# A list scheduler written in the kernel books two more costs: a wait of VectorE for GpSimd, and the overhead of a float32r product

## The chip, the cores and the metric

One core of one Trainium2 chip runs the whole step. The metric is device time in microseconds (us), from launch to the last output; the median of three runs is compared.

## What is computed

One inference step of a one-layer trunk for two groups of tokens that share the weights: a prompt of 1024 tokens, and a sample of 64 tokens that continues from stored states. Cut to what matters here:

```python
cols = x @ w_in + b_in                        # 1088 x 1024 by 1024 x 9864, float32
a_cols, a_z, b_qk, b_v, b_i, b_f, b_o, b_z, c_q, c_k, c_v, c_z, gates = split(cols)
# A: RWKV-7, 8 heads of 64: one state per head, token after token
S = S * w_t + sa_t (kk_t * a_t)^T + v_t k_t^T ;  sa_t = -S kk_t ;  y_t = S r_t
# B: mLSTM, 4 heads of 128, in chunks with a running maximum
# C: stick-breaking attention, 8 heads of 64, with a product over the keys between
ys  = stack([ya * silu(a_z), yb * silu(b_z), yc * silu(c_z)])
mix = sum(sigmoid(gates) * (ys @ w_branch)) @ w_out
x   = layer_norm(alpha * x + mix)
x   = x + (p @ w_ple) * sigmoid(x @ w_ple_gate)
```

The outputs are the new x of both groups, and the states of A, B and C.

## The kernel before

**Main stream.** The large products run as sums of three float32r products (high part by high part, low by high, high by low), function `three`. The 1088 tokens are cut into three groups of 384, 384 and 320 columns. A block is 128 columns of `w_in`: 8 steps of the contraction by 3 products by 3 groups, 72 products. 78 such blocks (5,592 products, as one of them needs 48) are followed by the merge with `w_branch` and by the tail. The main stream writes the PSUM banks `bk0` to `bk2`, which the order of instructions shows as bk_65 to bk_67, and reads the tiles `xh`, `xl` and `whl`.

**Side tasks.** The three mixers are written as Python generators, called tasks, and yield one operation at a time. A comes first: `a_front` prepares a pair of heads (bonus sums over `bd`, squared norms, scores), `a_inverses` solves triangular systems on GpSimd, 60 tensor_tensor instructions in a row for each of eight inverses, and `a_chain` carries the state: 17 chunks of 64 tokens for each of four pairs of heads, 68 chunks in all. One chunk of the chain goes like this: two products give `ry` (the first reads `V2`); VectorE and ScalarE copy them into `R1`; a product `u` reads `R1`; VectorE negates `u` into `uv2`, and ScalarE into `U2`; a product `zz` reads `uv2`, and VectorE forms the next state from it; a last product of the chunk reads `U2`. B and C follow, and `m_prep` readies the merge.

**What sets the order.** Every engine runs its instructions in the order in which the program issues them. That order is made while the program is built, by class `Sched`, a list scheduler. It keeps a clock for each engine and books every operation with a cost: `mm`, `tr`, `act`, `tt`, `ts`, `stt` and `cp` hold these cost formulas. The main stream books its products one after the other. After each step of `three` (three products), `poll` lets every side task issue the operation that it holds, if `when` says that this operation could start by the clock of TensorE. A side product is thus put into TensorE's queue at the step of the main stream at which the planner believes its inputs to be ready. If they are late on the chip, TensorE stands still, with the main stream's products behind it. `SLACK` is 0 for TensorE, so no reserve is planned.

Of the kernel before, what the change touches and what calls it, by code (L numbers as in the profile page):

```python
# [28 lines left out]
class Buf:  # L29
    def __init__(self, heap, off, n):  # L30
        self.heap, self.ap, self.off, self.n = heap, heap.ap[:, off:off + n], off, n
# [84 lines left out]


class Op:
    __slots__ = ("eng", "cost", "reads", "writes", "fn", "q", "load")

    def __init__(self, eng, cost, reads, writes, fn, q, load):
        self.eng, self.cost, self.reads, self.writes, self.fn, self.q, self.load = eng, cost, reads, writes, fn, q, load


class Sched:
# [3 lines left out]
    def __init__(self):  # L129
        self.clk = {"pe": 0.0, "act": 0.0, "dve": 0.0, "pool": 0.0, "s": 0.0, "dma": 0.0}  # L130
        self.tasks = []
        self.cur = self.main = Task(None, "main", main=True)
        self.idle = 0.0
        self.mem = {}
        self.log = None
        self.cache = {}
        self.shade = 0.0

    def note(self, what):
        if self.log is not None:  # L140
            self.log.append((round(self.clk["pe"] / 1000), what))
# [45 lines left out]
    def execute(self, op, at=0.0):  # L187
        if op.q:
            st = max(self.clk[op.q], self.dep(op), at)
            self.clk[op.q] = st + QUEUE[op.q]  # L190
            end = self.clk["dma"] = max(st + 1100.0, self.clk["dma"]) + op.cost
            done = end + 900.0
        else:
            st = max(self.clk[op.eng], self.dep(op), at)
            if op.load:
                st = max(st, self.clk["pe"] + op.load[0] - self.shade)
                self.shade = op.load[1]
            end = done = st + op.cost
            if op.eng == "pe":
                self.idle += st - self.clk["pe"]  # L200
            self.clk[op.eng] = end
        e = ENG[op.eng]
        for m, p, f in op.reads:
            np.maximum(m[0][1, p, f], end, out=m[0][1, p, f])
        end = done
        for m, p, f in op.writes:
            m[0][0, p, f] = end
            m[1][p, f] = e
        return op.fn()

    def emit(self, eng, cost, reads, writes, fn, q=None, load=None):
        op = Op(eng, cost, [self.region(a) for a in reads], [self.region(a) for a in writes], fn, q, load)
        if self.cur.main:
            return self.execute(op, self.clk["pe"] if eng == "dma" else 0.0)
        return op
# [80 lines left out]
def psum(ap):  # L296
    return "PSUM" in str(ap.space).upper()


def fsize(ap):  # L300
    n = 1
    for s in ap.shape[1:]:
        n *= s
    return n


class K:
# [5 lines left out]
    def mm(self, out, lhsT, rhs, start, stop, more=False):  # L313
        n, w = fsize(out), 0.82 * fsize(lhsT)
        if lhsT.dtype == F32R:
            c = d = 1 + (213.0 if n < 256 else n / 2.4)
        else:
            d = 1 + 2 * n / 2.4
            c = d + max(d, w)
        return self.S.emit("pe", c, [lhsT, rhs], [out],  # L320
                           lambda: self.nc.tensor.matmul(out, lhsT, rhs, start=start, stop=stop, skip_group_check=more),  # L321
                           load=(w, d))
# [32 lines left out]
    def tt(self, out, a, b, op, e="v"):  # L355
        if e == "v":
            return self.S.emit("dve", fsize(out) * 1.04 + 68, [a, b], [out],
                               lambda: self.nc.vector.tensor_tensor(out=out, in0=a, in1=b, op=op))  # L358
        return self.S.emit("pool", fsize(out) * 2.1 + 150, [a, b], [out],
                           lambda: self.nc.gpsimd.tensor_tensor(out=out, in0=a, in1=b, op=op))  # L360

    def ts(self, out, a, s1, op0, s2=None, op1=None, e="v"):
        kw = {"op1": op1} if op1 is not None else {}
        rd = [a] + [x for x in (s1, s2) if x is not None and not isinstance(x, (int, float))]
        q = self.nc.vector if e == "v" else self.nc.gpsimd
        if e == "v":
            c = fsize(out) * (1.04 if psum(a) else 0.52) + 68 + 62 * (len(rd) - 1)
        else:
            c = fsize(out) * (1.05 if (op0, op1) == (OP.mult, OP.add) else 2.33 + len(rd)) + 180
        return self.S.emit("dve" if e == "v" else "pool", c, rd, [out],  # L370
                           lambda: q.tensor_scalar(out=out, in0=a, scalar1=s1, scalar2=s2, op0=op0, **kw))  # L371

    def stt(self, out, a, s, b, op0, op1):
        rd = [a, b] + ([] if isinstance(s, float) else [s])
        return self.S.emit("dve", fsize(out) * 1.04 + 68 + 62 * (len(rd) - 2), rd, [out],
                           lambda: self.nc.vector.scalar_tensor_tensor(out=out, in0=a, scalar=s, in1=b, op0=op0, op1=op1))  # L376

    def cp(self, out, in_, e="v"):
        if e == "v":
            return self.S.emit("dve", fsize(out) * (1.04 if psum(in_) else 0.52) + 68, [in_], [out],  # L380
                               lambda: self.nc.vector.tensor_copy(out, in_))  # L381
        return self.S.emit("pool", fsize(out) * 3.4 + 120, [in_], [out], lambda: self.nc.gpsimd.tensor_copy(out, in_))

    def tr32(self, out, in_):
# [1874 lines left out]
```

## Time and profile before

| | us |
|---|---|
| median of 3 runs | 1745.0 (1744.7 to 1746.75) |
| the profiled execution | 1746.5 |
| span of its instructions | 1744.8 |
| TensorE (PE) busy | 1698.2, 97% of the span |
| VectorE (DVE) busy | 1159.4, 66% |
| ScalarE (ACT) busy | 791.5, 45% |
| GpSimd (POOL) busy | 452.1, 26% |

The profile draws a float32r product longer than the distance to the next one, because products overlap in the array; a busy TensorE is therefore not one without any loss. The granted TensorE clock is at its upper level, 2.4 GHz, in nearly the whole span.

### The profile page before, as it was taken

Reading aid. Unit: us, or ns where it says so; the run is one execution under the profiler, and the core shown is the slowest. Engines: PE = TensorE matmul, PEld = TensorE weight load, DVE = VectorE, ACT = ScalarE, POOL = GpSimd, SP = SyncE. Lnnn points to the kernel's source line nnn. Section 1 sums busy time; section 2 is a strip of 40 time slices with the busy share of each in tenths; the row PEclk is TensorE's granted clock in tenths of the full one; section 3 lists DMA queues with packets and bytes.
Section 4 is the critical chain, followed back from the end, with each engine's and each line's share of the span. In section 5 each row is a group of like instructions: output and inputs, shape, how many; then the busy total and the mean of one; then the engine's idle time right before and its main releaser. Section 6 shows DMA issues by size and latency. Waiting matters only on the chain.

```text
span 1744.8 us, 29994 instructions
## 1 busy us (share of the span) xinstructions
PE 1698.2 (97%) x10849; PEld 1582.7 (91%) x10849; DVE 1159.4 (66%) x2682; ACT 791.5 (45%) x1823; POOL 452.1 (26%) x951
## 2 busy tenths in 40 slices
PE   6999998999999999999999999999999999999999
PEld 5999987888888999999999999999999999988787
DVE  8766577677777656866743476867685568787743
ACT  6444454545455445544443655555654312222421
POOL 6005547075547441321202111212220000000100
PEclk9999999999999999999999999999999999999999
DMA  5543432323332333545424433343324877631421
GB/s 160 194 130 98 108 100 67 100 72 102 100 92 81 91 88 117 162 122 161 136 86 123 141 108 110 97 114 103 88 80 127 255 225 248 208 131 51 149 82 54
DMA packets 224634, 212.09 MB, mean 122 GB/s; under 512 B 53540, under 2 KB 192598, under 8 KB 224486
## 3 DMA queue, kind: packets, MB, share of 16 engines
q1 hardware_dynamic: 197518, 169.50, 32.8%
q10 hardware_dynamic: 22552, 29.02, 4.7%
q0 software_dynamic: 4416, 11.66, 2.2%
q8 instruction: 85, 1.39, 0.3%
q14 instruction: 63, 0.52, 0.1%
HBM read 136.81 MB, written 73.36 MB: 120 GB/s over the span
## 4 chain that ended last, share of the span: by engine, by line
PE 85%; DVE 8%; ACT 4%; issue 1%; DMA 1%; ACTq 0%; SPq 0%; POOL 0%; DVEq 0%
PE bk L321 80%; PE bk L328 5%; ACT heap L353 3%; DVE heap L376 2%; DVE heap L358 2%; DVE heap L371 1%; DVE whl L358 1%; DMA heap<-in_x_prompt_dram 1%; ACT whl L353 1%; DMA out_c_p_dram<-heap 0%; DVE heap L412 0%; DVE xl L358 0%; ACTq L431 0%; DVE heap L381 0%; DVE heap L409 0%
## 5 line engine op out<-in xcount | busy, mean ns | idle before, releaser
L321 PE MATMUL bk<-xh,whl 128*128 128x384 f32 (+1 forms) x3768 | 1051.9, 339 | 0.3 <-DVE heap L376 0.3
L321 PEld LDWEIGHTS bk<-xh,whl 128*128 128x128 f32 x3768 | 679.6, 188 | 10.0 <-issue 3.8
L321 PE MATMUL bk<-xl,whl 128*128 128x384 f32 (+3 forms) x2184 | 669.1, 328 | 1.4 <-POOL xl L360 0.8
L321 PEld LDWEIGHTS bk<-xl,whl 128*128 128x128 f32 (+1 forms) x2184 | 405.3, 189 | 4.9 <-POOL xl L360 1.5
L353 ACT ACTIVATE heap<-bk 64x64 f32<-64x64 f32 (+9 forms) x679 | 217.4, 335 | 348.1 <-PE bk L321 131.3
L360 POOL TENSOR_TENSOR heap<-heap 32x30 f32<-32x30 f32 (+14 forms) x480 | 266.1, 554 | 36.5
L358 DVE TENSOR_TENSOR whl<-heap,whl 128x1024 fp32r<-128x1024 f32 (+1 forms) x114 | 122.2, 1075 | 114.3 <-ACT whl L353 113.8
L328 PE MATMUL bk<-ident,heap 128*128 128x128 f32 (+3 forms) x942 | 177.3, 277 | 14.5 <-ACT heap L353 12.6
L358 DVE TENSOR_TENSOR heap<-heap 128x256 f32<-128x256 f32 (+18 forms) x372 | 174.8, 475 | 15.4 <-DMA heap<-yz 6.9
L321 PE MATMUL bk<-heap 128*128 128x128 f32 (+6 forms) x954 | 166.6, 290 | 11.7 <-ACT heap L353 9.8
L321 PEld LDWEIGHTS bk<-heap 128*128 128x128 f32 (+3 forms) x954 | 125.9, 180 | 37.7 <-ACT heap L353 23.8
L353 ACT ACTIVATE heap<-bk,pc 128x384 f32<-128x384 f32 (+5 forms) x218 | 113.9, 548 | 94.1 <-PE bk L321 66.0
L328 PEld LDWEIGHTS bk<-ident,heap 128*128 128x128 f32 (+3 forms) x942 | 119.9, 142 | 30.2 <-issue 15.5
L353 ACT ACTIVATE heap<-heap 64x64 f32<-64x64 f32 (+9 forms) x330 | 113.1, 348 | 66.5 <-DVE heap L376 28.1
L353 ACT ACTIVATE whl<-heap 128x1024 fp32r<-128x1024 f32 (+1 forms) x116 | 105.4, 912 | 73.0 <-PE bk L321 37.8
L321 PE MATMUL bk<-heapr 128*128 128x256 f32 (+2 forms) x524 | 123.0, 335 | 0.0
L353 ACT ACTIVATE heap<-bk,hb 128x384 f32<-128x384 f32 (+1 forms) x120 | 67.5, 563 | 121.3 <-PE bk L321 96.6
L321 PE MATMUL bk<-heap,heap 32*32 32x32 f32 (+2 forms) x990 | 111.7, 243 | 8.8 <-ACT heap L353 7.0
L321 PEld LDWEIGHTS bk<-heap,heap 128*128 128x128 f32 (+1 forms) x990 | 90.1, 152 | 26.9 <-ACT heap L353 17.4
L321 PE MATMUL bk<-heapr,whl 128*128 128x384 f32 (+2 forms) x648 | 113.9, 335 | 0.6 <-DVE heap L376 0.6
L376 DVE SCALAR_TENSOR_TENSOR heap<-heap 128x4 f32<-128x4 f32 (+8 forms) x259 | 81.4, 316 | 47.8 <-ACT heap L353 42.1
L321 PEld LDWEIGHTS bk<-heapr,whl 128*128 128x128 f32 x648 | 108.3, 188 | 4.1 <-issue 0.8
(154 smaller groups left out, 1795.3 us busy)
## 6 DMA issues: line engine op xcount, KB each, us to landing
heap<-in_w_in_dram SPq DMA_DIRECT2D x77, 512.0 KB
heap<-gt SPq DMA_DIRECT2D x24, 544.0 KB
gt<-heap ACTq DMA_DIRECT2D x48, 192.0 KB
heap<-crd SPq DMA_DIRECT2D x12, 544.0 KB
heap<-yd SPq DMA_DIRECT2D x24, 272.0 KB
heap<-yz SPq DMA_DIRECT2D x24, 272.0 KB
heap<-in_w_branch_dram SPq DMA_DIRECT2D x24, 256.0 KB
xsd<-heap SPq DMA_DIRECT2D x24, 192.0 KB
```

Source lines behind the costliest of these rows:

```text
L321: lambda: self.nc.tensor.matmul(out, lhsT, rhs, start=start, stop=stop, skip_group_check=more),
L328: lambda: self.nc.tensor.transpose(out, in_, self.ident[:p, :p]), load=(0.82 * fsize(in_), d))
L353: return self.nc.scalar.activation(out, in_, func, **kw)
L358: lambda: self.nc.vector.tensor_tensor(out=out, in0=a, in1=b, op=op))
L360: lambda: self.nc.gpsimd.tensor_tensor(out=out, in0=a, in1=b, op=op))
L371: lambda: q.tensor_scalar(out=out, in0=a, scalar1=s1, scalar2=s2, op0=op0, **kw))
L376: lambda: self.nc.vector.scalar_tensor_tensor(out=out, in0=a, scalar=s, in1=b, op0=op0, op1=op1))
```

## The change

Two costs of the planner change, and nothing else. First, a float32r product (`mm`) is booked with 13 ns beside its columns, where it was 1 ns. Second, a VectorE operation of the kinds `tt`, `ts`, `stt` and `cp` that reads no PSUM operand carries a flag `port`. When such an operation would be booked to start while a GpSimd operation is booked as running, its start is moved to the end of that operation. `pool` keeps the last 64 booked intervals of GpSimd. The same instructions are issued, in another order.

```diff
+        self.pool = []
...
+            if op.port:
+
+                for a, b in reversed(self.pool):
+                    if a <= st < b:
+                        st = b
+                        break
             end = done = st + op.cost
+            if op.eng == "pool":
+                self.pool = self.pool[-63:] + [(st, end)]
...
         if lhsT.dtype == F32R:
-            c = d = 1 + (213.0 if n < 256 else n / 2.4)
+            c = d = 13 + (213.0 if n < 256 else n / 2.4)
...
     def tt(self, out, a, b, op, e="v"):
         if e == "v":
             return self.S.emit("dve", fsize(out) * 1.04 + 68, [a, b], [out],
-                               lambda: self.nc.vector.tensor_tensor(out=out, in0=a, in1=b, op=op))
+                               lambda: self.nc.vector.tensor_tensor(out=out, in0=a, in1=b, op=op),
+                               port=not (psum(a) or psum(b)))
...
                            lambda: q.tensor_scalar(out=out, in0=a, scalar1=s1, scalar2=s2, op0=op0, **kw))
+                           port=e == "v" and not psum(a))
```

`stt` and `cp` get the flag in the same way as `tt`. What this does to the order is seen in one chunk of the chain, chunk 20 of 0 to 67 (the second pair of heads). The changed file has its product helper in line 331 and its transpose helper in line 338, where it was 321 and 328.

The first place is TensorE's queue from the first product of the chunk (it reads `V2` and writes `ry`, here bk_69 before and bk_68 after) to the product `u`, which reads `R1` (here bk_70 and bk_69). Rows with xh, xl and whl are main products; rows with ident are transposes; the row with bd is the bonus sum of `a_front`. Before the change:

```order
L321 MATMUL bk_69<-heap 128x128
L328 MATMUL bk_72<-ident,heap_76 128x128
L321 MATMUL bk_69<-heap,heap_76 128x128
L328 MATMUL bk_72<-ident,heap_76 128x128
L321 MATMUL bk_71<-heap_76,bd 128x256
L321 MATMUL bk_65<-xh,whl 128x384
L321 MATMUL bk_65<-xl,whl 128x384
L321 MATMUL bk_65<-xh,whl 128x384
L321 MATMUL bk_70<-heap 128x128
```

The same place after the change:

```order
L331 MATMUL bk_68<-heap 128x128
L331 MATMUL bk_68<-heap,heap_76 128x128
L331 MATMUL bk_65<-xh,whl 128x384
L331 MATMUL bk_65<-xl,whl 128x384
L331 MATMUL bk_65<-xh,whl 128x384 x2
L331 MATMUL bk_65<-xl,whl 128x384
L331 MATMUL bk_65<-xh,whl 128x384 x2
L331 MATMUL bk_65<-xl,whl 128x384
L331 MATMUL bk_65<-xh,whl 128x384
L331 MATMUL bk_69<-heap 128x128
```

Three main products, two transposes and the bonus sum stood between the two chain products; now nine main products stand there, and the bonus sum has moved to a later place.

The second place follows directly: TensorE's queue from behind the product `u` up to the product `zz` (it reads `uv2`). Before the change:

```order
L321 MATMUL bk_65<-xh,whl 128x384
L321 MATMUL bk_65<-xl,whl 128x384
L321 MATMUL bk_65<-xh,whl 128x384 x2
L321 MATMUL bk_65<-xl,whl 128x384
L321 MATMUL bk_65<-xh,whl 128x384 x2
L321 MATMUL bk_65<-xl,whl 128x384
L321 MATMUL bk_65<-xh,whl 128x384 x2
L321 MATMUL bk_65<-xl,whl 128x384
L321 MATMUL bk_65<-xh,whl 128x384
L321 MATMUL bk_70<-heap,heap_76 128x128
```

The same place after the change:

```order
L338 MATMUL bk_72<-ident,heap_76 128x128 x2
L331 MATMUL bk_66<-xh,whl 128x384
L331 MATMUL bk_66<-xl,whl 128x384
L331 MATMUL bk_66<-xh,whl 128x384 x2
L331 MATMUL bk_66<-xl,whl 128x384
L331 MATMUL bk_66<-xh,whl 128x384
L331 MATMUL bk_69<-heap,heap_76 128x128
```

Twelve main products stood between `u` and `zz`; now six stand there, and two transposes.

## Rows read from the trace of the kernel before

**Rows 1.** The page: span, and busy time of each engine.
```profile
span 1744.8 us, 29994 instructions
PE 1698.2 (97%) x10849; PEld 1582.7 (91%) x10849; DVE 1159.4 (66%) x2682; ACT 791.5 (45%) x1823; POOL 452.1 (26%) x951
```

**Rows 2.** Busy time by stretch: A, C, merge and tail (columns in the first row).
```profile
core 0: us, PE busy (x) PEld busy (x) DVE busy (x) ACT busy (x) POOL busy (x), PEclk, DMA share, GB/s
0.00:100.00 100.00, 84.73 (x501) 79.52 (x502) 78.50 (x166) 51.66 (x96) 34.59 (x60) 1.00 0.56 179
...
300.00:400.00 100.00, 93.30 (x653) 84.32 (x652) 71.69 (x270) 50.64 (x155) 40.51 (x77) 1.00 0.33 90
...
1000.00:1100.00 100.00, 100.00 (x659) 94.79 (x657) 72.13 (x83) 59.84 (x113) 20.80 (x64) 1.00 0.35 104
1100.00:1200.00 100.00, 100.00 (x672) 96.45 (x671) 71.21 (x82) 55.52 (x105) 19.24 (x55) 1.00 0.34 101
1200.00:1300.00 100.00, 99.64 (x661) 95.36 (x661) 74.65 (x85) 58.98 (x112) 23.23 (x62) 1.00 0.33 99
1300.00:1400.00 100.00, 100.00 (x635) 99.47 (x634) 54.40 (x75) 34.68 (x57) 2.08 (x8) 1.00 0.57 181
...
1600.00:1745.00 145.00, 140.59 (x639) 112.96 (x637) 77.53 (x151) 42.60 (x80) 5.38 (x10) 0.99 0.28 90
```

**Rows 3.** GpSimd's timeline, 260 to 412 us: start, length, instructions, idle time before.
```profile
265.84 38.76 POOL L360 TENSOR_TENSOR heap<-heap 32x30 f32<-32x30 f32 x60
...
347.34 38.69 POOL L360 TENSOR_TENSOR heap<-heap 36x30 f32<-36x30 f32 x60
```

**Rows 4.** Busy time in the eight stretches of an inverse: one, and the sum.
```profile
347.00:386.00 39.00, 34.74 (x226) 31.32 (x225) 31.02 (x94) 19.38 (x62) 34.11 (x61) 1.00 0.18 56
...
sum 312.00, PE 291.33 PEld 261.21 DVE 223.13 ACT 154.98 POOL 272.03; mean PE 36.42 PEld 32.65 DVE 27.89 ACT 19.37 POOL 34.00
```

**Rows 5.** The same for the eight stretches without an inverse, 186 to 670 us: sum.
```profile
sum 211.00, PE 207.72 PEld 195.88 DVE 136.78 ACT 103.71 POOL 7.10; mean PE 25.97 PEld 24.49 DVE 17.10 ACT 12.96 POOL 0.89
```

**Rows 6.** VectorE's groups, 347 to 386 us, during an inverse: busy us, mean ns.
```profile
L358 DVE TENSOR_TENSOR heap<-heap 128x256 f32<-128x256 f32 x10 | 5.2, 518 | 0.6 <-ACT heap L353 0.5
L376 DVE SCALAR_TENSOR_TENSOR heap<-bk,heap 64x64 f32<-64x64 f32 x12 | 3.4, 283 | 0.9 <-PE bk L321 0.7
L371 DVE TENSOR_SCALAR heap<-heap 128x128 f32<-128x128 f32 x7 | 3.1, 437 | 0.1
```

**Rows 7.** The same groups, 305.5 to 346.5 us, without an inverse.
```profile
L376 DVE SCALAR_TENSOR_TENSOR heap<-bk,heap 64x64 f32<-64x64 f32 x10 | 2.8, 284 | 1.9 <-PE bk L321 1.8
...
L358 DVE TENSOR_TENSOR heap<-heap 128x256 f32<-128x256 f32 x4 | 1.6, 412 | 0.0
...
L371 DVE TENSOR_SCALAR heap<-heap 128x128 f32<-128x128 f32 x4 | 1.1, 284 | 0.6 <-ACT heap L353 0.6
```

**Rows 8.** The timeline of chunk 20, 363.8 to 370 us.
```profile
364.80 0.96 DVE L376 SCALAR_TENSOR_TENSOR heap<-heap,pc,heap 128x128 f32<-128x128 f32 x2
365.80 0.22 DVE L381 COPY heap<-bk 64x64 f32<-64x64 f32 x1
365.82 0.30 PEld L321 LDWEIGHTS bk<-heap,bd 128*128 128x128 f32 x2 [1.11 <-DVE heap L376]
365.82 0.70 PE L321 MATMUL bk<-heap,bd 128*128 128x256 f32 x2 [0.87 <-DVE heap L376]
...
369.57 0.49 PE L321 MATMUL bk<-heap,heap 128*128 128x128 f32 x2 [0.22 <-ACT heap L353]
```

**Rows 9.** TensorE's waits, 160 to 620 us: who ended them, us, times, longest.
```profile
PE bk L321 <- ACT heap L353: 16.5, 34, 1.6
PE bk L321 <- DVE heap L376: 6.0, 7, 1.7
```

**Rows 10.** The chain that ended last: its longest piece, in the merge.
```profile
1330.43 132.94 PE bk L321 x810
```

More of the change, by code (lines that the diff above doesn't have):

```diff
@@ L118, with __init__ @@
 class Op:
-    __slots__ = ("eng", "cost", "reads", "writes", "fn", "q", "load")
-    def __init__(self, eng, cost, reads, writes, fn, q, load):
+    __slots__ = ("eng", "cost", "reads", "writes", "fn", "q", "load", "port")
+    def __init__(self, eng, cost, reads, writes, fn, q, load, port):
         self.eng, self.cost, self.reads, self.writes, self.fn, self.q, self.load = eng, cost, reads, writes, fn, q, load
+        self.port = port
 class Sched:
@@ L209, in execute, with emit @@
         return op.fn()
-    def emit(self, eng, cost, reads, writes, fn, q=None, load=None):
-        op = Op(eng, cost, [self.region(a) for a in reads], [self.region(a) for a in writes], fn, q, load)
+    def emit(self, eng, cost, reads, writes, fn, q=None, load=None, port=False):
+        op = Op(eng, cost, [self.region(a) for a in reads], [self.region(a) for a in writes], fn, q, load, port)
         if self.cur.main:
@@ L370, in ts @@
         return self.S.emit("dve" if e == "v" else "pool", c, rd, [out],
-                           lambda: q.tensor_scalar(out=out, in0=a, scalar1=s1, scalar2=s2, op0=op0, **kw))
+                           lambda: q.tensor_scalar(out=out, in0=a, scalar1=s1, scalar2=s2, op0=op0, **kw),
+                           port=e == "v" and not psum(a))
     def stt(self, out, a, s, b, op0, op1):
@@ L375, in stt @@
         return self.S.emit("dve", fsize(out) * 1.04 + 68 + 62 * (len(rd) - 2), rd, [out],
-                           lambda: self.nc.vector.scalar_tensor_tensor(out=out, in0=a, scalar=s, in1=b, op0=op0, op1=op1))
+                           lambda: self.nc.vector.scalar_tensor_tensor(out=out, in0=a, scalar=s, in1=b, op0=op0, op1=op1),
+                           port=not (psum(a) or psum(b)))
     def cp(self, out, in_, e="v"):
@@ L380, in cp @@
             return self.S.emit("dve", fsize(out) * (1.04 if psum(in_) else 0.52) + 68, [in_], [out],
-                               lambda: self.nc.vector.tensor_copy(out, in_))
+                               lambda: self.nc.vector.tensor_copy(out, in_), port=not psum(in_))
         return self.S.emit("pool", fsize(out) * 3.4 + 120, [in_], [out], lambda: self.nc.gpsimd.tensor_copy(out, in_))
```

## The prediction

> **What bounds the kernel now.** I read the page first, then TensorE's busy time by stretch, then the waits. TensorE is busy for 1698.2 of 1744.8 us [rows 1], so 46.6 us are all that a better order can win outright. The stretches say where they lie [rows 2]. 15.3 us are in the first 100 us and 4.4 us in the last 145; there the order is written out by hand, or is the tail's. In the C stage, from 1000 to 1300 us, TensorE stands still for 0.4 us in 300, and in the merge for nothing. What is left lies in the A stage: 6.7 us between 300 and 400 us alone.
>
> The A stage falls into two kinds of stretches. An inverse keeps GpSimd running for 38.7 us with 60 instructions back to back [rows 3], and there are eight of them. In the eight stretches with an inverse TensorE is busy for 291.33 of 312 us, so it idles for 20.7 us, 6.6% [rows 4]. In the stretches between them it idles for 3.3 of 211 us, 1.6% [rows 5]. The reader should see that the same side tasks cost TensorE four times as much idle time while GpSimd runs.
>
> VectorE shows why. Between two float32 operands in SBUF, a 128x256 tensor_tensor takes 518 ns during an inverse and 412 ns without one; a 128x128 tensor_scalar takes 437 and 284 ns. An operation of the same engine that reads PSUM (64x64) takes 283 and 284 ns [rows 6, 7]. So VectorE loses 106 to 153 ns per operation without a PSUM operand while GpSimd runs, and nothing on the others. The planner before books none of this. Chunk 20 shows the result: two such operations take 0.96 us, the bonus product on TensorE waits 1.11 us for them, and the copy into `R1` starts behind them [rows 8]. ScalarE ends more of TensorE's waits than VectorE does (16.5 against 6.0 us, [rows 9]), but its copies for the chain are themselves released by products that VectorE held up.
>
> **The change part by part.** The number of instructions on each engine is the same before and after (9,861 products and transposes on TensorE); no operation, transfer or buffer is added. Neighbours of a float32r and a float32 product or a transpose, where a weight load is exposed, number 671 before and 665 after on TensorE's queue, so that nothing is to be had or lost there. All of the effect is in waits.
>
> *The flag `port`.* Its largest possible gain is that the stretches of an inverse come down to the idle share of the others: 20.7 us less 1.6% of 312 us, which is 20.7 - 4.9 = 15.8 us. A wait under some 0.17 us doesn't show as idle time, since a product is drawn longer than the step to the next; by the weight loads' idle time, which shows it, the same sum is 50.8 - 22.4 = 28.4 us (312 - 261.21, less 7.2% from 195.88 of 211). That is the outer bound. How much of it is had depends on whether more TensorE work now lies between the chain's products. In the first place shown in the order, nine main products lie between the chain's products where three lay with the bonus sum; but in the second, six where twelve lay.
>
> *The 12 ns.* They are right: 810 main products of the merge take 132.94 us, 164.1 ns each [rows 10], and the columns (384, 384, 320 at 2.4 GHz, mean 151.1) with 13 ns make 164.1. The planner before booked 152.1. But the error was a reserve. It put every side product behind as many main products as fill the latency by its own count, and each of them then took 12 ns more than booked: with six to nine products under a wait, some 70 to 110 ns of reserve for every one. With the right cost it is gone. Main products come in threes (0.49 us), so what changes is how often one group of three fewer is placed.
>
> I counted this on TensorE's queue. From the chain's first product to `u` lie 6.8 main products on average before and 6.6 after (three or fewer in 15, now 21, of 68 chunks); from `u` to the last product 8.8 and 9.2 (three or fewer in 11, now 8). Within a run of chunks (fewer than 45 main products from one chunk to the next) it is 19.8 per chunk before (61 chunks) and 19.2 after (59). The two corrections thus nearly cancel in the mean: work isn't added to the chain's waits, it is shared out otherwise, more to those that GpSimd holds up and less to the others. So I take three tenths of the 15.8 us, -4.7 us: nearer to nothing than to all, because the mean cover doesn't grow, but not nothing, because the planner now knows which waits are long.
>
> The price is paid in the stretches without an inverse. About half of the chain's 204 waits, 100, lie there; at six products each loses up to 72 ns, 7.2 us if all ran dry at once. They idle for only 1.6% now, so most have room: a fifth, +1.4 us. In the C stage 75 products of the value sums wait for the evacuation of a transpose; 10.6 main products lie in between before, 9.6 after, so 75 x 0.16 = 12 us is the outer price, and nothing the inner one. With 0.4 us of idle time in 300 there is room now, and I take +0.5 us.
>
> *What is free.* The side tasks end earlier in the main stream: the last side product ahead of the merge stands behind main product 4,989 where it stood behind 5,385 of 5,592. Nothing waits for that: TensorE is fully busy from 1300 us on [rows 2], and only the margin of 207 products, 34 us, becomes 603. What hides the removed wait's successor is the main stream; if a side product is still late, the main products queued behind it wait with it, as before.
>
> Sum: -4.7 + 1.4 + 0.5 = -2.8 us. The profiled execution took 1746.5 us, 1.7 us above its span; 1743.7 us follow for it. It lies 1.5 us above the median of the runs, 1745.0, so that the median comes to some 1742 us.
>
> **A rule beside it.** The order's flag makes VectorE wait to the end of GpSimd's instruction. An instruction of the inverse starts every 645 ns (38.69 us by 60, [rows 3]), so that a wait to its end is some 320 ns from a random start, and the rows show 106 to 153. The planner would book about twice what is lost, which gives more cover than needed: rival 1. The Trainium skill, "SBUF — State Buffer", section "SBUF: two separate sides", states the booked rule: the pair of ports that VectorE and GpSimd share is locked for a whole instruction, and the loser blocks fully. The trace agrees on which operations lose, but shows less than half of that wait as longer duration. By that rule alone the gain would be some 9.4 us, twice the 4.7.
>
> **The rivals.** *Rival 1: the flag pays in full.* Booking twice the loss puts enough work under the held-up waits, and six tenths or all of the 15.8 us come back: 1729 to 1737 us. For it: GpSimd's stretches hold most of the idle time. Against it: the mean cover doesn't grow.
>
> *Rival 2: nothing moves.* Gain and price are equal, 1743 to 1747 us. For it: the counts 19.8 and 19.2, and 6.8 and 6.6. Against: the spread between the two kinds of stretches is fourfold, and an even cancelling would be chance.
>
> *Rival 3: slower, because the reserve is gone.* The mechanism is the 12 ns alone, at the chain's first wait: the copy into `R1` leaves by one group of three less in more chunks (21 of 68 with three or fewer). If half of the outer prices fall due, 3.6 us in the quiet stretches and 6 us in the C stage, and the flag wins 1 us, the sum is +8.6, 1753.6 us; it decides, above 1748.5, from the point where a quarter of the outer prices fall due (4.5 of 19.2 us). For it: the planner has no slack for TensorE. Against it: the C stage idles for 0.1% now.
>
> **How the numbers follow.** A measurement of this kernel can tell 0.2%, 3.5 us, from no change: below 1741.5 is faster, above 1748.5 slower. Forecast (1738 to 1745 us): 0.40, about half of it below 1741.5. Rival 1: 0.18. Rival 2: 0.19. Rival 3: 0.23, nearly all above 1748.5. So faster 0.20 + 0.18 = 0.38; same 0.20 + 0.19 = 0.39; slower 0.23. The predicted time is 1742 us. The range reaches halfway into rival 1 and to most of rival 3: 1732 to 1752 us.
>
> **What would show it.** If the steps are right, TensorE's idle share in the stretches of an inverse falls from 6.6% to some 5%, that of the others rises from 1.6% towards 2%, and 1000 to 1300 us of the C stage stays under 1 us of idle time. VectorE's 437 and 518 ns stay as they are, since the loss itself isn't removed. The prediction is wrong if the inverse's stretches idle for less than 3% (rival 1), or if the C stage or the quiet stretches show several us of new waits for ScalarE (rival 3). A gain or a loss outside of the A and C stages would belong to none of these.

## The result, and the profile after

The changed kernel is slower: 1760.9 us (median of 4 runs, 1757.0 to 1763.7) against 1745.7 us before (1744.7 to 1746.8), ratio 1.0081 with an interval of 1.0068 to 1.0094. The forecast was 1742 us, 1732 to 1752: wrong, and on the other side. The profiled execution took 1757.0 us; its trace shows 10.5 of the 15.2 us.

The page of the changed kernel, span and busy time of each engine (beside [rows 1]):

```profile
span 1755.3 us, 30000 instructions
PE 1706.3 (97%) x10849; PEld 1585.1 (90%) x10849; DVE 1153.0 (66%) x2682; ACT 792.2 (45%) x1823; POOL 448.9 (26%) x951
```

The span has grown by 10.5 us. Busy time by stretch says where. First the changed kernel's eight stretches with an inverse, one of them and the sum, which answer to [rows 4]:

```profile
335.00:372.00 37.00, 33.41 (x215) 29.85 (x214) 29.12 (x96) 18.55 (x59) 32.33 (x61) 1.00 0.24 71
...
sum 302.00, PE 282.60 PEld 253.53 DVE 213.40 ACT 146.05 POOL 265.05; mean PE 35.33 PEld 31.69 DVE 26.68 ACT 18.26 POOL 33.13
```

and the sum of its eight stretches without an inverse, 180 to 674 us, for [rows 5]:

```profile
sum 231.00, PE 224.32 PEld 207.28 DVE 142.80 ACT 117.50 POOL 13.05; mean PE 28.04 PEld 25.91 DVE 17.85 ACT 14.69 POOL 1.63
```

TensorE idles for 19.4 of 302 us with an inverse (6.4%, before 6.6%) and for 6.7 of 231 us without one (2.9%, before 1.6%). Put together, the stages A (160 to 720 us), B (720 to 1000) and C (1000 to 1300) of the kernel before:

```profile
160.00:720.00 560.00, 535.61 (x3848) 492.14 (x3848) 383.22 (x1219) 280.71 (x817) 278.81 (x528) 1.00 0.34 96
720.00:1000.00 280.00, 278.20 (x1789) 270.75 (x1788) 160.62 (x430) 127.87 (x288) 53.66 (x134) 0.99 0.42 131
1000.00:1300.00 300.00, 299.64 (x1987) 286.61 (x1986) 217.99 (x248) 174.34 (x328) 63.27 (x180) 1.00 0.34 101
```

and of the changed one:

```profile
160.00:720.00 560.00, 533.61 (x3803) 486.45 (x3802) 372.81 (x1205) 277.69 (x811) 267.60 (x519) 1.00 0.33 94
720.00:1000.00 280.00, 277.25 (x1793) 266.99 (x1793) 186.09 (x459) 138.80 (x317) 61.02 (x157) 0.99 0.43 134
1000.00:1300.00 300.00, 299.62 (x1983) 287.01 (x1982) 213.78 (x249) 172.85 (x318) 58.99 (x161) 1.00 0.36 105
```

The second number behind each length is TensorE's busy time, the third that of its weight loads. Matmul rows hide short waits, since a product is drawn longer than its step; the weight loads' idle time shows them. In A it grows from 67.9 to 73.5 us and in B from 9.3 to 13.0, 9.4 us together. In C it falls by 0.4. So some 9 of the 10.5 us are waits of the A and B stages.

Who is waited for there, TensorE's waits from 160 to 1000 us (total us, times, longest), before:

```profile
PE bk L321 <- ACT heap L353: 16.8, 35, 1.6
PE bk L321 <- DVE heap L376: 7.7, 10, 1.7
```

and after:

```profile
PE bk L331 <- ACT heap L363: 22.9, 41, 1.8
PE bk L331 <- DVE heap L388: 4.3, 4, 2.6
```

The waits for VectorE have shrunk by 3.4 us, those for ScalarE have grown by 6.1. One wait has a sequel; the changed kernel's timeline of TensorE at 782.6 us, and its windows around it:

```profile
782.60 0.43 PE L331 MATMUL bk<-heap,heap 64*64 64x129 f32 x2 [2.55 <-DVE heap L388]
```

```profile
700.00:780.00 80.00, 79.52 (x533) 77.61 (x531) 63.51 (x154) 38.84 (x95) 22.54 (x51) 1.00 0.53 161
780.00:784.00 4.00, 1.45 (x8) 0.86 (x7) 2.22 (x10) 1.23 (x5) 0.00 (x0) 0.96 0.01 4
784.00:791.00 7.00, 7.00 (x28) 6.63 (x28) 2.67 (x13) 3.17 (x9) 2.40 (x13) 0.53 0.38 122
791.00:800.00 9.00, 9.00 (x61) 9.00 (x60) 7.02 (x34) 3.14 (x11) 0.00 (x0) 1.00 0.55 197
```

Behind 2.55 us of idle time the granted clock (the third number from the end of a row) is 0.53 of full speed for the next 7 us, that is mostly at 1.2 GHz, and TensorE runs 4 instructions per us there where it runs nearly 7 at full clock.

### The profile page after: what moved, and what is told of

It is laid out like the page before. It is cut to its first block, busy times and chain, and to the rows that moved or that the text cites. A ratio compares the mean times of both kernels' runs of the same rounds, so it can differ in the third digit from the quotient of the medians.

```text
span 1755.3 us, 30000 instructions
## 1 busy us (share of the span) xinstructions
PE 1706.3 (97%) x10849; PEld 1585.1 (90%) x10849; DVE 1153.0 (66%) x2682; ACT 792.2 (45%) x1823; POOL 448.9 (26%) x951
## 4 chain that ended last, share of the span: by engine, by line
PE 81%; DVE 9%; ACT 5%; DMA 2%; issue 2%; SPq 0%; ACTq 0%; POOL 0%; DVEq 0%; POOLq 0%
PE bk L331 75%; PE bk L338 6%; ACT heap L363 4%; DVE heap L388 3%; DVE heap L368 2%; DVE heap L382 2%; DVE whl L368 1%; ACT whl L363 1%; DMA heap<-in_x_prompt_dram 1%; DMA heap<-gd 1%; DVE heap L425 0%; SPq L444 0%; DVE heap L394 0%; DVE heap L414 0%; ACTq L444 0%
## 5 line engine op out<-in xcount | busy, mean ns | idle before, releaser
L363 ACT ACTIVATE heap<-bk 64x64 f32<-64x64 f32 (+12 forms) x679 | 217.7, 335 | 353.0 <-PE bk L331 134.2
L338 PE MATMUL bk<-ident,heap 128*128 128x128 f32 (+3 forms) x942 | 177.3, 278 | 14.0 <-ACT heap L363 12.4
L331 PE MATMUL bk<-heap 128*128 128x128 f32 (+7 forms) x946 | 166.6, 293 | 15.6 <-ACT heap L363 13.9
L368 DVE TENSOR_TENSOR heap<-heap 128x256 f32<-128x256 f32 (+19 forms) x358 | 166.3, 470 | 15.2 <-DMA heap<-yz 5.0
L331 PEld LDWEIGHTS bk<-heap 128*128 128x128 f32 (+2 forms) x946 | 124.4, 181 | 42.7 <-ACT heap L363 30.9
L331 PE MATMUL bk<-heap,heap 128*128 128x128 f32 (+2 forms) x998 | 115.8, 244 | 13.2 <-ACT heap L363 9.1
L388 DVE SCALAR_TENSOR_TENSOR heap<-heap 128x4 f32<-128x4 f32 (+9 forms) x266 | 90.3, 342 | 53.5 <-ACT heap L363 47.0
L331 PEld LDWEIGHTS bk<-heap,heap 128*128 128x128 f32 (+1 forms) x998 | 93.2, 153 | 34.1 <-ACT heap L363 21.1
```

Source lines behind the costliest of these rows:

```text
L338: lambda: self.nc.tensor.transpose(out, in_, self.ident[:p, :p]), load=(0.82 * fsize(in_), d))
L363: return self.nc.scalar.activation(out, in_, func, **kw)
```

## The experiments

The theory formed from this trace: the two edits work against each other, and both are large. The flag books a longer wait for VectorE, so that more main products lie under the chain's products; the 12 ns take such cover away everywhere. The rivals are that one of them does nothing, and, later, that any changed number deals out the order anew with a scatter of this size.

Two readings carry the verdicts. One is TensorE's idle time in the A stage, 160 to 720 us, straight from the rows. The other is the loss up to main product 2,800 (or up to the last one, 5,592), of which some expectations speak: the time at which that product starts in the trace, less the durations of all of TensorE's work queued ahead of it, each taken as fixed. This is a reckoning and no row of a view, so it stands beside rows and run times, and differences of it under some 3 us say little. Before, it is 39.9 us at product 2,800 and 57.9 at 5,592; after, 47.2 and 69.2.

**One edit alone.** `e1_flag_only` keeps the flag and books 1 ns; `e2_overhead_only` books 13 ns and drops the flag.

```diff
 e1_flag_only
-            c = d = 13 + (213.0 if n < 256 else n / 2.4)
+            c = d = 1 + (213.0 if n < 256 else n / 2.4)
 e2_overhead_only
-            if op.port:
+            if False and op.port:
```

> The flag for VectorE's wait is kept, a float32r product is booked with 1 ns again. Theory 1 (the 12 ns took the reserve under the waits, the flag itself is good): 1735 to 1744 us, faster than before, with less idle TensorE time in the stretches of an inverse (under 5%) and 1.6% or less between them. Theory 2 (the flag costs, since it shifts work to the wrong waits): 1755 us or more, like both together. Theory 3 (any new order lands somewhere else by luck): no telling, within 10 us of before on either side.

> No flag, a float32r product is booked with 13 ns. Theory 1: slower than both together, 1765 to 1775 us, because nothing pays back; idle share between the inverses 3% or more, and during them above 6.6%. Theory 2: 1740 to 1748 us, as before. Theory 3: within 10 us of before on either side.

`e1_flag_only`: 1749.6 us, ratio 1.0024 (1.0015 to 1.0033). `e2_overhead_only`: 1777.3 us, ratio 1.0181 (1.0162 to 1.0200). The first is 6 us above the range of theory 1, the second 2 us above it. A, and the stretch in which the merge's products begin, 1340 to 1400 us and ten of it, with the flag alone:

```profile
160.00:720.00 560.00, 545.41 (x3922) 505.22 (x3921) 371.40 (x1194) 279.37 (x809) 284.08 (x534) 1.00 0.34 97
...
1340.00:1400.00 60.00, 50.55 (x253) 44.20 (x253) 32.42 (x51) 15.72 (x26) 0.00 (x0) 0.83 0.70 224
...
1360.00:1370.00 10.00, 5.47 (x11) 2.56 (x10) 4.80 (x8) 2.62 (x4) 0.00 (x0) 0.50 0.72 220
```

and A and B with the 12 ns alone:

```profile
160.00:720.00 560.00, 523.87 (x3695) 474.26 (x3696) 378.67 (x1218) 274.63 (x811) 272.97 (x522) 0.99 0.33 93
720.00:1000.00 280.00, 276.70 (x1795) 265.50 (x1794) 194.49 (x453) 145.05 (x320) 61.85 (x157) 1.00 0.41 130
```

In the A stage TensorE idles for 24.4 us before, 14.6 with the flag alone, 36.1 with the 12 ns alone, and 26.4 with both. The eight stretches with an inverse and the eight without one, with the flag alone:

```profile
sum 309.50, PE 297.62 PEld 273.64 DVE 212.22 ACT 153.39 POOL 272.83; mean PE 37.20 PEld 34.20 DVE 26.53 ACT 19.17 POOL 34.10
sum 224.60, PE 222.22 PEld 207.37 DVE 143.12 ACT 111.99 POOL 9.76; mean PE 27.78 PEld 25.92 DVE 17.89 ACT 14.00 POOL 1.22
```

and with the 12 ns alone:

```profile
sum 309.90, PE 281.59 PEld 249.35 DVE 217.82 ACT 147.66 POOL 273.05; mean PE 35.20 PEld 31.17 DVE 27.23 ACT 18.46 POOL 34.13
sum 213.80, PE 209.19 PEld 194.44 DVE 141.41 ACT 107.45 POOL 8.00; mean PE 26.15 PEld 24.30 DVE 17.68 ACT 13.43 POOL 1.00
```

The flag alone brings TensorE's idle time with an inverse down to 11.9 us (3.8%, before 20.7), the 12 ns alone bring it up to 28.3 us (9.1%). Without an inverse it is 2.4 us (1.1%) and 4.6 us (2.2%, where 3% or more was expected), before 3.3. The losses up to main product 5,592 are 57.9, 41.7, 88.7 and 69.2 us. The flag is thus worth 16 us without the 12 ns and 19.5 with them, the 12 ns cost 31 and 28: the two nearly add up, and neither is small. The run times alone say nearly the same where the end of the side tasks doesn't disturb: 1777.3 less 1745.7 is 31.6 us for the 12 ns without the flag, 1777.3 less 1760.9 is 16.4 us for the flag with them.

The flag alone is nevertheless slower than before, and its loss is at another place. Its last side product stands behind main product 5,553 (before 5,385, after 4,989; in TensorE's queue all such places of this document lie 9 products earlier, here 5,544, 5,376 and 4,980, in every kernel alike, so that no comparison changes), and the stretch from 1340 us, which was fully busy before [rows 2], idles. TensorE's timeline with the flag alone:

```profile
1358.42 1.77 PE L331 MATMUL bk<-heapr,whl 128*128 128x384 f32 x3 [2.20 <-ACT heapr L363]
1360.80 1.77 PE L331 MATMUL bk<-heapr,whl 128*128 128x384 f32 x3 [0.61 <-ACT heapr L363]
```

The merge's products take their operands as the last side tasks deliver them, three at a time, and the granted clock is 0.50 from 1360 to 1370 us (0.83 over the 60 us). That costs 9.5 us of idle time and, by the loss as reckoned above, some 19 us behind main product 5,592 beyond the 8 us of before. The theory of two large effects stands; the end of the side tasks is the third thing that counts, which I had priced at nothing.

**A reserve for every side product.** `e3_both_reserve100` and `e4_before_reserve100` hold each side product back by 100 ns, in the changed kernel and in the kernel before.

```diff
-SLACK = {"pe": 0.0, "act": 250.0, "dve": 250.0, "pool": 250.0, "dma": 0.0}
+SLACK = {"pe": -100.0, "act": 250.0, "dve": 250.0, "pool": 250.0, "dma": 0.0}
```

> Both corrections, and a side operation of TensorE is issued only when the planner believes its inputs to be 100 ns old (SLACK of TensorE -100). Theory 1: the reserve is back, in plain sight; 1738 to 1746 us, TensorE's granted clock 0.999 again. Theory 2 and 3: no reason for a gain, 1752 to 1765 us.

> The costs of before (1 ns, no flag), and 100 ns of reserve for TensorE's side operations. Theory 1: a reserve also helps the planner of before, which has some 70 to 110 ns already: 1733 to 1742 us. Theory 2: no change, 1742 to 1748 us. Theory 3: within 10 us of before on either side.

1815.4 us, ratio 1.0402 (1.0370 to 1.0433), and 1832.0 us, 1.0484 (1.0452 to 1.0516): the slowest of all, and outside of what any theory expected. The A stage of `e3_both_reserve100`:

```profile
160.00:720.00 560.00, 548.15 (x3624) 478.61 (x3623) 347.66 (x1120) 253.10 (x745) 262.41 (x493) 0.97 0.31 85
```

Its idle time did fall, to 11.9 us, but fewer instructions were done in the same time (3,624 against 3,803), and the weight loads idle for 81.4 us. Held back one by one, the side products no longer stand in groups: on TensorE's queue, places where a float32 product or a transpose follows a float32r one rise from 665 to 1,059 (from 671 to 1,052 in the kernel before). The weight loads' idle time shows little of the loss, though: in A it is 8 us more than in the changed kernel, while the profiled execution of `e3_both_reserve100` is 61 us longer. The side tasks now outlast the main stream. Side products still stand behind its last product, 5,592; the merge starts 11.3 us after the start of that product in `e3_both_reserve100` and 54.7 us after it in `e4_before_reserve100`, where it was 0.15 us in the two kernels without this reserve. `e4_before_reserve100` from 1400 us:

```profile
1400.00:1434.00 34.00, 21.12 (x99) 16.52 (x97) 17.21 (x22) 10.84 (x20) 0.67 (x4) 0.75 0.13 41
1434.00:1480.00 46.00, 38.35 (x170) 31.61 (x170) 28.51 (x46) 11.59 (x18) 0.00 (x0) 0.74 0.75 243
```

TensorE idles for 20.5 of these 80 us, the granted clock is 0.74 to 0.75, and in the A stage of both kernels the clock is 0.97. What the parted groups cost by themselves is not shown. This pair could not test the theory, since the end of the side tasks swamps it, and doses of the two edits' own numbers had to.

**The 12 ns by stage.** `h1_13_after_A` and `h2_13_in_C` keep the flag and book 13 ns only once the A chains, or A and B, are through; `h8_13_in_A_only` does the opposite; `h7_noflag_13_after_A` is h1 without the flag; `h4_1_7_13` books 1, 7 and 13 ns in the three stages.

```diff
-            c = d = 13 + (213.0 if n < 256 else n / 2.4)
+            o = 1 if self.acdone < 4 else 13     # h1, h7
+            o = 1 if self.bdone < 4 else 13      # h2
+            o = 13 if self.acdone < 4 else 1     # h8
+            c = d = o + (213.0 if n < 256 else n / 2.4)
```

> The flag throughout; a float32r product is booked with 1 ns while the A chains run, with 13 ns after them. Theory 1 (the 12 ns cost waits in A and B, the flag saves 16 us in A, and the side tasks' end must come before the main stream's): A loses as little as with the flag alone, 33 us at main product 2,400 where before lost 42; the last side product stands at main product 5,265, so that no wait ahead of the merge is left; B pays 4 to 7 us; 1732 to 1738 us. Rival (the gain of the flag alone was luck, or is given back at the end whatever one does): 1743 to 1750 us.

> As the one before, but 13 ns only when the B tasks are done too, so that C alone is issued faster; C showed no price for the 12 ns. The last side product stands at main product 5,355, against 5,385 before and 5,553 with the flag alone. Theory 1: 1727 to 1732 us, no idle TensorE ahead of the merge. Rival: 1743 to 1750 us.

> No flag; 1 ns while the A chains run, 13 ns after them. Theory 1: A exactly as before (the same order up to its end), B pays 4 to 7 us, C nothing: 1747 to 1752 us. Rival (the 12 ns cost their price in C or behind it): 1760 us or more.

> The flag, with 13 ns booked for a float32r product until the last chain of the A stage is through, and 1 ns from there on. Theory (the 12 ns cost waits in A itself, some 22 us by main product 2,800, on top of what the flag saves; nothing in C): it loses as much as the changed kernel up to main product 2,800, then as little as the flag alone in B and C, and its side tasks are through before the merge (last side product behind main product 5,223): 1747 to 1753 us. Rival (the prediction's place for the price, the quiet stretches and the C stage, with A's gain kept): 1730 to 1737 us.

> The flag, with 1 ns in the A stage, 7 ns in B and 13 ns in C. Theory (the price lies in A's waits, the end of the side tasks ahead of the merge is what 13 ns give back later): as the version with 13 ns behind A, 1731 to 1738 us, no wait of the merge, last side product behind main product 5,205. Rival (each ns booked costs its share in any stage): 4 us above that version, 1739 us or more.

| | us | ratio to before | last side product behind |
|---|---|---|---|
| h1 | 1734.4 | 0.9923 (0.9896 to 0.9950) | 5,265 |
| h2 | 1736.8 | 0.9938 (0.9916 to 0.9961) | 5,355 |
| h4 | 1731.9 | 0.9916 (0.9901 to 0.9932) | 5,205 |
| h7 | 1750.3 | 1.0014 (1.0001 to 1.0027) | 5,121 |
| h8 | 1756.3 | 1.0055 (1.0036 to 1.0075) | 5,223 |

A of `h1_13_after_A` and its stretch ahead of the merge:

```profile
160.00:720.00 560.00, 545.44 (x3928) 504.68 (x3927) 372.59 (x1194) 279.97 (x811) 283.02 (x534) 1.00 0.34 97
...
1340.00:1400.00 60.00, 60.00 (x368) 60.00 (x367) 27.23 (x47) 13.32 (x22) 0.00 (x0) 1.00 0.56 183
```

A, B and C of `h7_noflag_13_after_A`:

```profile
160.00:720.00 560.00, 535.78 (x3845) 491.95 (x3844) 382.33 (x1217) 281.79 (x817) 278.25 (x527) 1.00 0.34 96
720.00:1000.00 280.00, 278.93 (x1819) 268.00 (x1818) 187.44 (x460) 141.61 (x317) 59.99 (x158) 1.00 0.44 135
1000.00:1300.00 300.00, 297.19 (x1964) 284.00 (x1964) 208.81 (x242) 168.34 (x312) 60.86 (x160) 1.00 0.32 95
```

A and B of `h8_13_in_A_only`:

```profile
160.00:720.00 560.00, 534.96 (x3783) 487.10 (x3783) 369.52 (x1197) 276.29 (x808) 268.75 (x520) 0.99 0.33 92
720.00:1000.00 280.00, 277.29 (x1784) 267.57 (x1783) 175.15 (x456) 135.62 (x308) 54.66 (x148) 0.99 0.43 133
```

h1 has A as with the flag alone (14.6 us idle) and no wait ahead of the merge: there the 13 ns pull the side tasks forward, from main product 5,553 to 5,265, because fewer main products go under each of them. h7 has A as before the change (24.2 against 24.4 us) and ends 4 us later than before: its weight loads idle for 2.8 us more in B (12.0) and 2.6 more in C (16.0). h8 idles for 25.0 us in A, about as the changed kernel, and with 1 ns in B and C is still slow: the price lies in A. It came out 3 us above its expectation; its weight loads idle for 12.4 us in B (280 less 267.57), 2.5 us more than with the flag alone, although both book 1 ns there; the rival's 1730 to 1737 us is far off. h2 missed its expectation by some 5 us: between main products 4,000 and 5,592 it loses 13.8 us where the flag alone loses 7.4, and its weight loads idle for 14.9 us in C where those of the flag alone idle for 10.6, so that the 13 ns have a price in C too.

**Doses.** If cover is the cause, values between must lie between. `h5_flag_5` books 5 ns in all stages; `d2_flag_9`, `d3_noflag_5` and `d8_flag_minus_5` book their number in A, then 7 and 13. `h10_rest_160`, `d5_rest_80`, `d6_rest_plus_160` and `d7_rest_plus_320` book 1 ns in A, then 13 (h10) or 7 and 13 (the others), and shift the end of the wait that the flag books; `d9_plus_160_minus_5` does both.

```diff
-                        st = b
+                        st = max(st, b - 160.0)      # h10; d5: b - 80, d6: b + 160, d7: b + 320
```

> The flag, and 5 ns for a float32r product in all stages: a third of the step from 1 to 13. Last side product at 5,181. Theory 1: a third of the price of 28 us, 9 us, and the flag's 16 us, no wait at the end: 1735 to 1740 us. If the price comes only with the full cost (a threshold and no dose), 1728 to 1732 us; if any step off 1 ns costs it all, 1755 us or more.

> The version with 1 ns in A and 13 ns behind it, but the flag books 160 ns less than the rest of GpSimd's instruction, which is about what the trace of the changed kernel shows VectorE to lose. Theory (the flag's worth is the knowledge of which waits are long; their size matters little): 1731 to 1738 us, and the main products up to 2,400 lose 30 to 36 us as in the version with the whole rest. Rival (the cover that the double price buys is what the flag's 16 us are made of): half of the gain goes, 1740 to 1744 us.

> The flag, with 9 ns booked for a float32r product in the A stage, 7 in B, 13 in C. Theory 1 (each ns that is booked takes reserve from A's waits, in proportion): up to main product 2,800 it loses some 40 us, between 24 us at 1 ns and 47 us at 13 ns, and takes 1744 to 1751 us. Theory 2 (a change of any number deals out the order anew, by chance): the loss lies anywhere between 25 and 50 us, without an order by size. A loss of over 47 or of under 32 us (that at 5 ns) speaks for theory 2.

> No flag, 5 ns in the A stage, 7 in B, 13 in C. Theory 1 (in proportion): up to main product 2,800 it loses some 49 us, a third of the way from 40 us at 1 ns to 69 us at 13 ns, and takes 1751 to 1757 us. Theory 2 (chance): the loss lies anywhere between 35 and 70 us; under 40 or over 60 us speaks for it.

> The version with 1, 7 and 13 ns (1731.9 us), but the flag books 80 ns less than the rest of GpSimd's instruction. Theory 1 (what the flag gains grows with the wait that it books): up to main product 2,800 it loses some 33 us, halfway between 24 us with the whole rest and 42 us with 160 ns less, and takes 1738 to 1744 us. Theory 2 (chance): the loss lies anywhere between 24 and 45 us; under 27 or over 42 us speaks for it.

> The version with 1, 7 and 13 ns (1731.9 us), but the flag books 160 ns more than the rest of GpSimd's instruction. Theory 1 (what the flag gains grows with the wait that it books): up to main product 2,800 it loses under 24 us, and takes 1722 to 1731 us. Theory 2 (chance, or a best value at the whole rest): it loses more than 27 us there and takes 1735 us or more.

> As the version with 160 ns more than the rest of GpSimd's instruction (1726.7 us), with 320 ns more. Theory 1 (cover in proportion to the wait that is booked, until TensorE hardly waits): up to main product 2,800 it loses 8 to 14 us, 2 to 8 us less than with 160 ns more; the side tasks end later (last side product behind main product 5,436), still ahead of the merge: 1719 to 1726 us. Rival (the cover is enough at 160 ns more, and the later side tasks only cost): 1727 us or more.

> The flag with the whole rest, and minus 5 ns booked for a float32r product in the A stage (6 less than 1 ns), 7 in B, 13 in C. Theory 1 (some 2 us for each ns): up to main product 2,800 it loses some 12 us where 1 ns loses 24; last side product behind main product 5,352, no wait of the merge: 1717 to 1725 us. Rival (1 ns is the best value, what lies below gives back in held-up side tasks): 1730 us or more.

> Both reserves: 160 ns more than the rest, and minus 5 ns in the A stage. Theory (the reserve's gain ends where the side tasks come too late for the merge): up to main product 2,800 it loses under 12 us, but its last side product stands behind main product 5,568 of 5,592, and TensorE waits in the stretch from 1340 to 1380 us and runs there at half clock, as with the flag alone (5,553): 15 to 20 us are lost there, 1733 to 1745 us. Rival (the end of the side tasks does not matter): under 1724 us.

The A stage, in this order: `h10_rest_160`, `d5_rest_80`, `d6_rest_plus_160`, `d7_rest_plus_320`,

```profile
160.00:720.00 560.00, 539.05 (x3815) 493.54 (x3813) 362.18 (x1174) 272.82 (x791) 272.54 (x516) 0.99 0.33 92
```

```profile
160.00:720.00 560.00, 541.52 (x3845) 498.01 (x3844) 362.60 (x1174) 273.24 (x790) 273.93 (x516) 0.99 0.33 92
```

```profile
160.00:720.00 560.00, 553.01 (x3978) 515.06 (x3977) 378.35 (x1202) 284.17 (x816) 277.12 (x521) 1.00 0.34 96
```

```profile
160.00:720.00 560.00, 554.05 (x3975) 519.18 (x3973) 357.85 (x1149) 276.06 (x790) 277.04 (x521) 1.00 0.34 96
```

and the B stage of `d7_rest_plus_320`, then of `d8_flag_minus_5`:

```profile
720.00:1000.00 280.00, 276.85 (x1806) 268.23 (x1805) 182.61 (x499) 137.84 (x321) 58.25 (x139) 1.00 0.44 138
```

```profile
720.00:1000.00 280.00, 277.73 (x1803) 268.49 (x1802) 183.50 (x478) 139.08 (x322) 57.90 (x154) 1.00 0.44 139
```

The A stage of `d8_flag_minus_5`, `h5_flag_5`, `d2_flag_9` and `d3_noflag_5`, in this order:

```profile
160.00:720.00 560.00, 550.38 (x3960) 512.50 (x3959) 363.78 (x1190) 280.08 (x807) 278.99 (x530) 1.00 0.34 96
```

```profile
160.00:720.00 560.00, 542.75 (x3886) 500.63 (x3886) 371.50 (x1190) 281.01 (x808) 280.47 (x530) 1.00 0.34 96
```

```profile
160.00:720.00 560.00, 538.89 (x3828) 490.57 (x3827) 369.06 (x1190) 276.55 (x804) 268.88 (x515) 1.00 0.33 93
```

```profile
160.00:720.00 560.00, 530.40 (x3786) 486.82 (x3784) 368.07 (x1182) 275.26 (x805) 278.41 (x526) 0.99 0.34 94
```

| booked for VectorE's wait | booked ns in A | idle in A | loss at 2,800 | us | ratio to before |
|---|---|---|---|---|---|
| nothing (before) | 1 | 24.4 | 39.9 | | 1 |
| nothing (d3) | 5 | 29.6 | 51.3 | 1756.5 | 1.0065 (1.0047 to 1.0084) |
| nothing (e2) | 13 | 36.1 | 68.6 | 1777.3 | 1.0181 |
| rest - 160 ns (h10) | 1 | 21.0 | 42.3 | 1753.5 | 1.0044 (1.0027 to 1.0061) |
| rest - 80 ns (d5) | 1 | 18.5 | 35.2 | 1745.1 | 0.9987 (0.9976 to 0.9997) |
| rest (h4) | 1 | 14.9 | 24.0 | 1731.9 | 0.9916 |
| rest + 160 ns (d6) | 1 | 7.0 | 15.8 | 1726.7 | 0.9889 (0.9870 to 0.9907) |
| rest + 320 ns (d7) | 1 | 6.0 | 20.3 | 1727.7 | 0.9898 (0.9883 to 0.9913) |
| rest (d8) | -5 | 9.6 | 24.7 | 1726.8 | 0.9893 (0.9878 to 0.9907) |
| rest (h5) | 5 | 17.3 | 32.2 | 1744.9 | 0.9987 (0.9972 to 1.0001) |
| rest (d2) | 9 | 21.1 | 41.4 | 1750.1 | 1.0025 (1.0016 to 1.0035) |
| rest (after) | 13 | 26.4 | 47.2 | 1760.9 | 1.0081 |

"Rest" is the rest of GpSimd's running instruction. The idle time in A stands in the order of what is booked, in all three series (the flag's wait at 1 ns, the ns with the flag, the ns without it), without an exception. Scatter doesn't do that: theory 2 of these expectations, chance, falls. `h10_rest_160` fell past even its rival's 1744 us: with 160 ns less, nothing of the flag's gain is left in the loss, and it is no faster than h7, the same kernel without the flag (1753.5 against 1750.3 us). `d2_flag_9`, `d3_noflag_5` and `d6_rest_plus_160` came out within theory 1's ranges, `d5_rest_80` 1 us and `h5_flag_5` 5 us above them; the B stage of h5, which books 5 ns there too, idles for 4.4 us, and why is open. With the flag each ns costs some 1.9 us by the loss at product 2,800 ((47.2 - 24.0) by 12), without it 2.4 ((68.6 - 39.9) by 12).

Below 1 ns (d8) and above 160 ns (d7) the idle time in A still falls, but the run time falls less than expected (d8, 5 us below h4) or not at all (d7, against d6). Both missed their expectations by some 2 us; d7's 1727.7 us is the time of its rival (enough cover at 160 ns more). The loss up to product 2,800 of these two, 20.3 and 24.7 us, is no good measure beside the others: 36 of the small 32x32 products that stand ahead of product 2,800 in d6 and h4 stand behind it in d7 and d8, and the reckoning, by its own differences, takes off some 8 us for them, though a run of 18 of them takes 0.69 us in the trace of d6. Product 2,800 itself starts at 685.6 us in h4, 676.0 in d6, 670.5 in d7 and 675.6 in d8. With 3 to 4 us of such other work ahead, an estimate from the steps in the traces, the loss falls on, by some 2 us from d6 to d7 and by 6 from h4 to d8. Some of it is given back later: the B stage idles for 3.2 us in d7 and 2.3 in d8, against 0.7 in d6 and 0.1 in h4.

Both reserves together (`d9_plus_160_minus_5`), A and the stretch ahead of the merge:

```profile
160.00:720.00 560.00, 549.51 (x3955) 512.38 (x3954) 362.16 (x1163) 277.43 (x797) 277.92 (x532) 1.00 0.35 98
...
1340.00:1400.00 60.00, 48.76 (x238) 41.85 (x237) 30.87 (x50) 15.19 (x25) 0.00 (x0) 0.80 0.70 221
```

1750.0 us, ratio 1.0025 (1.0013 to 1.0037): the last side product stands behind main product 5,568, and the wait of the flag alone is back (11.2 us idle, clock 0.80); it came out 5 us slower even than expected. Nor do the two reserves add up in A: its idle time is 10.5 us, where +160 ns alone has 7.0 and -5 ns alone 9.6. The fastest versions, `d6_rest_plus_160` and `d8_flag_minus_5` at 1726.7 and 1726.8 us, beat both kernels, the one before by some 20 us; their last side products stand behind main products 5,355 and 5,352.

## Why the prediction was wrong, step by step

**What bounds the kernel.** Right: the waits of the A stage were where time could be had, and VectorE's loss behind GpSimd is not removed. The changed kernel's groups of VectorE at 335 to 372 us, with an inverse (for [rows 6]):

```profile
L382 DVE TENSOR_SCALAR heap<-heap 128x128 f32<-128x128 f32 x6 | 3.6, 595 | 0.0
L368 DVE TENSOR_TENSOR heap<-heap 128x256 f32<-128x256 f32 x7 | 3.5, 511 | 0.6 <-ACT heap L363 0.5
L388 DVE SCALAR_TENSOR_TENSOR heap<-bk,heap 64x64 f32<-64x64 f32 x12 | 3.4, 283 | 2.7 <-PE bk L331 2.6
```

and at 303 to 335 us, without one (for [rows 7]):

```profile
L368 DVE TENSOR_TENSOR heap<-heap 128x256 f32<-128x256 f32 x7 | 2.9, 416 | 0.1
L388 DVE SCALAR_TENSOR_TENSOR heap<-bk,heap 64x64 f32<-64x64 f32 x8 | 2.3, 284 | 2.2 <-PE bk L331 2.1
...
L382 DVE TENSOR_SCALAR heap<-heap 128x128 f32<-128x128 f32 x4 | 1.1, 281 | 0.8 <-ACT heap L363 0.7
```

The tensor_tensor loses 95 ns and the six tensor_scalar here 314 (153 before, so that this loss has a wide spread); what reads PSUM loses nothing. The idle shares forecast (some 5% with an inverse, towards 2% without, under 1 us in C) came out at 6.4%, 2.9% and 0.4 us: only the last was right.

**The flag, -4.7 us.** Mis-sized. By itself it is worth 16 us of waits, of which the prediction allowed 4.7. In the terms of its bound, 15.8 us of idle time in the stretches with an inverse, it is worth 8.8 us (20.7 to 11.9), more than half of the bound and not three tenths.

**The 12 ns, +1.4 and +0.5 us.** This is the step that failed. They cost 28 to 31 us. The mechanism was named (a reserve is gone), but it was priced for half of the chain's waits and for the C stage. It acts on waits all over A, those with an inverse too, and on those of B: A's idle time grows by 12 us with the flag and without it (14.6 to 26.4, 24.4 to 36.1). The larger part lies in the stretches with an inverse, where the prediction put no price: 7.6 us without the flag (20.7 to 28.3) and 7.5 with it (11.9 to 19.4), against 1.3 (3.3 to 4.6) and 4.3 (2.4 to 6.7) in the quiet ones. The outer price for the quiet stretches, 7.2 us, was no bound, since it counted 72 ns for 100 waits of the chain and nothing for those of the bonus sums, the fronts and the B stage.

**"The two corrections thus nearly cancel in the mean".** The count was right and its reading wrong. Main products per chunk within a run were 19.8 before and 19.2 after; with the flag alone they are 21.6, with the 12 ns alone 18.8, with the fastest version 21.9. The prediction read 19.8 to 19.2 as no change, though 0.6 products by 164.1 ns [rows 10] by 59 chunks are already 5.8 us less work under the chain's waits, and took a gain on top of it. The count had the right sign here, but is no measure: it is 20.5 at 9 ns with the flag, 19.9 at 5 and 20.1 at -5, and 22.4 in the slowest kernel of all, `e4_before_reserve100`.

**"Nothing waits for that."** True of this change, which ends the side tasks earlier, but no law: their end is worth nothing only as long as it lies ahead of the merge. The flag alone moves it from 5,385 to 5,553 and loses some 19 us there, and with a reserve for every side product it lies behind the main stream altogether.

**Rival 3** named the mechanism (1753.6 us) with the wrong places and a third of the price; in the changed kernel C idles no longer than before, as the prediction's argument against it said, though its weight loads idle for 2.4 us more than with the flag alone (13.0 against 10.6). Rival 1's reason, that booking twice the loss puts enough work under the held-up waits, is what the doses show to be right: with 160 ns less than the rest, nearer to what VectorE loses, nothing of the gain is left (1753.5 us, where h1, the same with the whole rest, took 1734.4). It fell with the 12 ns, which it priced like the forecast. The rule beside it ("SBUF — State Buffer", section "SBUF: two separate sides", of the Trainium skill) thus gave the better number to book, though the rows show less than that wait as longer duration: cover pays beyond the mean loss, here up to 160 ns beyond the whole rest.

**What stays open.** The changed kernel's other runs are 3 to 7 us longer than its profiled one, at a mean granted clock of 0.993 to 0.995 against 0.997; no trace of them says where it fell. Why the cost is 1.9 to 2.4 us for each ns was not taken apart wait by wait, so that it is argued, and not counted, which waits make it up.

## What to carry to other kernels

In an order made by a planner, an error in a booked cost can be the reserve that hides every wait; before correcting it, find the waits that it covers and put a reserve back where the loss lies. When two edits are said to cancel, price each alone; a count of what lies under the waits is no price. A stream that runs off behind the critical one is free only up to the point where its end is needed: keep that point (here the last side product, which must lie ahead of the merge) in view in every variant.

## What the runs showed of the hardware that was not expected

Behind short idle spells of TensorE its granted clock fell in several places. In the changed kernel 2.55 us of waiting at 780 us are followed by 7 us at 0.53 of full speed, and with the flag alone the stretch from 1340 us, in which it waits again and again, runs at 0.83 on average. In `e4_before_reserve100` it is some 0.75 of full speed from 1400 to 1480 us, where TensorE idles for 20.5 of 80 us. In these places a wait cost more than its own length.
